# Latent queries summed in half a bank without a join, rotary halves shuffled, and three early tiles of the first gate

## The chip, the cores and the metric

One core of one Trainium2 chip runs the whole program. The metric is the device time of one execution, in microseconds. Before the change it is 2838.24 us, the median of 3 runs (2837.36 to 2838.51).

## The reference

A bidirectional encoder of two layers over 256 tokens of width 2048, in f32. Each layer projects the normed input into queries, keys and values of a differential attention, into two low-rank latents and a shared rotary key of a latent attention, and into two gates. Cut to what the change touches:

```python
h = rmsnorm(x, g_mix[i])
z = h @ w_in[i]
dq, dk, dv, cq, ckv, kr, ga, gb = jnp.split(z, split_at, axis=-1)
# differential attention: 8 heads -> od -> y_diff
qf = (rmsnorm(cq, g_q_latent[i]) @ w_q_up[i]).reshape(b, s, MLA_HEADS, 128 + 64)
q_nope = qf[..., :128]
q_rope = apply_rope(qf[..., 128:], cos_m, sin_m)
...
k_rope = apply_rope(kr[:, :, None, :], cos_m, sin_m)[:, :, 0, :]
om = latent_attention(q_nope, q_rope, k_nope, k_rope, v_mla)
merged = jax.nn.sigmoid(ga) * y_diff + jax.nn.sigmoid(gb) * y_mla
x = x + merged @ w_out[i]
# then a SwiGLU block and a gated embedding block
```

`apply_rope` rotates the first half of the 64 rotary features against the second half.

## The kernel before, in words

**Products.** Activations lie with features on the 128 partitions and the 256 tokens (`T`) along them, and every matmul operand is kept as a high and a low part: `u[:, :T]` and `u[:, T:]`. A weight tile comes by DMA in pieces of 8 blocks of 128 x 128 (`piece`); the scalar engine (ACT) rounds it into `whi`, the vector engine (DVE) writes the rest into `wlo`. `emit` then issues two matmuls for a block: `whi` against all 512 columns of the operand (high and low part side by side, into both halves of a PSUM bank), and `wlo` against the 256 high columns, into the second half. So the result lies in two halves, and `joined` adds them: ACT copies the second half into a scratch `join`, DVE adds the first half and writes a scratch `a` (four buffers). From then on the bank is free.

**Banks.** Products take one of four banks named `mm` (values `mmv` take the same four); transposes, small products and head outputs take two banks named `at`; scores take two banks named `S`.

**Latent queries.** `queries_up(n)` makes two tiles of `w_q_up` from one piece (`pair`), each from 4 blocks. Tiles 0 to 7 are the heads' unrotated parts; each is split into the operand `qn[n]`, which lies in the slot `fa(n)`. That slot holds the output `od[n]` of differential head n until `settle` has scaled and transposed it (a product with `ident` into an `at` bank, then a split into `ub`). Tiles 8 to 11 hold the rotary parts of two heads each; `rotated` multiplies them with a 128 x 128 matrix `swap` on the tensor engine (PE) to exchange the halves. The shared key goes through `swaps` and `halves` in the same way.

**Settling.** `settle(4)` scales `od[4]` to `od[7]`. Its factor is computed for the four heads at once by `rsqrt`, a chain of eleven small DVE operations (`rv`, `ry`, `ra`) on the sums of squares `ssd`, so it starts when head 7 is done.

**Gates.** 16 tiles of each gate (`wga`, `wgb`), 16 blocks each, fill PE's time beside the heads of the latent attention: two before each next head, `wga` there, `wgb` after it. Tile n of the first gate is stored in the slot `fa(n // 2)`, when the head's query that lies there has been used.

**Order.** All this is written as a program in order; a scheduler then puts each engine's instructions into a fixed order. Each engine works its own list strictly in that order, so an instruction that waits holds up all that stand behind it on its engine.

Of the kernel before, what the change touches and what calls it, by code (L numbers as in the profile page):

```python
# [12 lines left out]
F32 = mybir.dt.float32  # L13
# [26 lines left out]
BOTH = 6  # L40
PAD = 96 - 64 - 8
STEP = 48
NO_SYNC = mybir.DependencyInfo(mybir.DependencyClass.NoSync, mybir.DependencyReason.DATA)

TWO_PI = 2.0 * math.pi
# [8 lines left out]
def encoder(ctx, tc, x, p, positions, cols, lams, wq, wk, wv, wcq, wckv, wkr, wga, wgb,  # L54
            w_q_up, w_kn, w_v, w_bd, w_bm, w_out, w_gate, w_up, w_down, w_pin, w_pg, rope_c, out):
    nc = tc.nc
    V, A, PE = nc.vector, nc.scalar, nc.tensor
# [13 lines left out]
    def bank(ps=ps_at, tag="at", name="at", shape=(P, 2 * T)):  # L71
        return ps.tile(list(shape), F32, tag=tag, name=name)

    def tt(o, a, b, op):
        return V.tensor_tensor(out=o, in0=a, in1=b, op=op)  # L75
# [26 lines left out]
    at = 0  # L102
# [16 lines left out]
    swap, swaps, halves = (rc[:, 4 + j * P : 4 + (j + 1) * P] for j in range(3))  # L119
    aside = [fa(j) for j in range(5)]  # L120
    posi = aside[0][:, 0, :].bitcast(I32)
    posf = aside[0][:, 1, :]
# [86 lines left out]
    def emit(acc, hi, lo, at, us, first, last, inside=None):  # L209
        for j, u in enumerate(us):  # L210
            s, start, stop = slice((at + j) * P, (at + j + 1) * P), first and j == 0, last and j == len(us) - 1
            lead = PE.matmul(acc, hi[:, s], u, start=start, stop=False)  # L212
# [3 lines left out]
            rest = PE.matmul(acc[:, T:], lo[:, s], u[:, :T], start=False, stop=stop)  # L216
            if inside and inside[0] == j:
                tc.keep_in_program_order(rest)
# [9 lines left out]
            emit(acc, hi, lo, 0, us[a : a + m], a == 0, a + m == n, inside and (inside[0] - a, inside[1]))  # L228
        return acc

    def pair(src, us):

        n = len(us)
        hi, lo = piece(src.rearrange("n p m -> p n m"), 2 * n)
        for j in range(2):
            acc = bank(ps_mm, "mm", "mm")
            emit(acc, hi, lo, j * n, us, True, True)
            yield acc

    def joined(acc, o=None):  # L240
        t = scratch("join", 3)
        A.activation(t, acc[:, T:], AF.Copy)  # L242
        o = scratch("a", 4) if o is None else o
        tt(o, acc[:, :T], t, ALU.add)
        return o

    def split(u, src, gain=None):
        hi, lo = u[:, :T], u[:, T:]
        if gain is None:
            return A.activation(hi, src, AF.Copy), tt(lo, src, hi.bitcast(F32), ALU.subtract)  # L250
        return A.activation(hi, src, AF.Copy, scale=gain), stt(lo, src, gain, hi.bitcast(F32), ALU.mult, ALU.subtract)
# [109 lines left out]
        nc.gpsimd.memset(t.bitcast(F32), 0.0)  # L361

    def rotated(a, c_, s_, o=None):
        r = bank()
        if o is None:
            PE.matmul(r[:, T:], halves, a, start=True, stop=True)
        PE.matmul(r[:, :T], swap if o is not None else swaps, a, start=True, stop=True)  # L367
        t = scratch("sh", 2)
        tt(t, r[:, :T], s_, ALU.mult)
        tt(a, a if o is not None else r[:, T:], c_, ALU.mult)  # L370
        tt(a, a, t, ALU.add)
        if o is None:
            for j, t in enumerate(krs):
                split(t[64 * j : 64 * j + 64], a[64 * j : 64 * j + 64])
        else:
            split(o, a)
# [59 lines left out]
        return tmp.tile([P, 2, T], dt, tag=tag, name=tag, bufs=2)  # L436

    last_exp = [None]
    ROPE16 = [(j + 8) if j < 8 else (j - 8) if j < 16 else j for j in range(32)]

    def values(src, us, load=None):
# [43 lines left out]
    for L in range(DEPTH):  # L485
# [64 lines left out]
                split(kn[-1], joined(acc))  # L550

        def queries_up(n):
            for acc in pair(w_q_up[L, n : n + 2], cq):
                if n < MH:
                    qn.append(operand(fa(len(qn), F32R)))
                    split(qn[-1], joined(acc))
                else:
                    if n > MH:
                        qr.append(operand(fc(len(qr) - 2, F32R)))
                    at = qr[len(qr) - 1] if n > MH else qr[ropes[0]]  # L560
                    rotated(joined(acc), cos_m, sin_m, at)
                    ropes[0] += 1

        ropes = [0]
# [8 lines left out]
        def beside():  # L573

            for h in range(2, DH):
                if h < 6:
                    keys_up(2 * h - 4)
                elif h == 7:
                    rotated(joined(narrow(wkr[L], ua)), crm, srm)
                yield  # L580
                queries_keys(h)
                yield
            settle(0)
            for n in (8, 0, 2, 10):
                queries_up(n)
                yield
            settle(4)
            for n in (4, 6):
                queries_up(n)

        def gate(w, store, n):
            tt(store(n), joined(product(w[L, n], ua)), R, ALU.mult)

        def gate_a(n):
            if n % 2 == 0:
                gas.append(fa(n // 2))
            return gas[n // 2][:, n % 2, :]

        def gate_b(n):
            if n % 2 == 0:  # L600
                gbs.append(fb(n // 2))
            return gbs[n // 2][:, n % 2, :]

        gas, gbs = [], []

        def sigmoid(sg):
            si = A.activation(sg, sg, AF.Sigmoid)
# [57 lines left out]


        oms = ub[8:]
        todo = iter(range(NC))

        def mla_weights(h):  # L670
            E = weights()
            S, = scores(three(qn[h], kn[h]) + three(qr[h // 2], krs[h % 2]))
# [16 lines left out]
                    PE.matmul(o[:, :T], a[:, kb, :], b[:, kb, :], start=kb + j == 0, stop=kb + j == 3)  # L689
            split(oms[h], o[:, :T])  # L690

        pipelined(mla_weights, mla_out, MH, lambda: gate(wga, gate_a, next(todo)))


        for n in range(NC):
            gate(wgb, gate_b, n)
        ms = ua
        for n in range(NC):
            ga, gb = (t[n // 2][:, n % 2, :] for t in (gas, gbs))
# [186 lines left out]
        ("g_q_latent0", 4), ("g_q_latent1", 4), ("g_kv_latent0", 2), ("g_kv_latent1", 2), ("g_subln", 2)]  # L886


def rope_constants():


    c = np.zeros((P, 4 + 3 * P), np.float32)
    f32 = np.float32
    for base, dim in ((0, 16), (2, 64)):
        inv = f32(THETA) ** (-np.arange(0, dim, 2, dtype=f32) / f32(dim))
        for q in range(P):
            d = q % 64
            if d < dim:
                c[q, base] = inv[d % (dim // 2)]
                c[q, base + 1] = -1.0 if d < dim // 2 else 1.0  # L900
    for q in range(P):
        c[q, 4 + (q ^ 32)] = 1.0
        for m in (q, q ^ 64):
            c[q, 4 + P + (m ^ 32)] = 1.0
            c[q, 4 + 2 * P + m] = 1.0
    return c


# [18 lines left out]
def laid_out(a):  # L927
    a = {k: np.asarray(v) for k, v in a.items()}
    w_in = a["w_in"]
    cut = np.cumsum([0, 1024, 1024, 1024, QR, KVR, 64, DM, DM])  # L930
    z = [w_in[:, :, cut[j] : cut[j + 1]] for j in range(8)]
    up = a["w_q_up"].reshape(DEPTH, QR, MH, 192)
    kv = a["w_kv_up"].reshape(DEPTH, KVR, MH, 256)
    flat = lambda w: w.reshape(w.shape[0], w.shape[1], -1)
    named = {f"{n}{i}": a[n][i] for n in ("g_mix", "g_ffn", "g_ple", "g_q_latent", "g_kv_latent") for i in range(DEPTH)}
    named["g_final"] = a["g_final"]
    named["g_subln"] = a["g_subln"]
    return {
        "x": np.ascontiguousarray(a["x"][0].T.reshape(NC, P, T).transpose(1, 0, 2)),
        "p": np.ascontiguousarray(a["p"][:, 0].transpose(0, 2, 1).reshape(DEPTH, 2, P, T).transpose(0, 2, 1, 3)),  # L940
        "positions": np.ascontiguousarray(a["positions"]),
        "cols": np.ascontiguousarray(np.concatenate([columns(named[n]) for n, _ in COLS], axis=1)),
        "lams": np.ascontiguousarray(np.stack([a["lambda_q1"], a["lambda_q2"], a["lambda_k1"], a["lambda_k2"]], axis=1).reshape(1, -1)),
        "wq": tiles(z[0]), "wk": tiles(z[1]), "wv": wide(z[2]), "wcq": tiles(z[3]), "wckv": tiles(z[4]),
        "wkr": np.ascontiguousarray(z[5].reshape(DEPTH, NC, P, 64).transpose(0, 2, 1, 3)).reshape(DEPTH, P, NC * 64), "wga": tiles(z[6]), "wgb": tiles(z[7]),
        "w_q_up": tiles(np.concatenate([flat(up[..., :128]), flat(up[..., 128:])], axis=2)),
        "w_kn": tiles(flat(kv[..., :128])), "w_v": wide(flat(kv[..., 128:])),
        "w_bd": tiles(a["w_branch_diff"]), "w_bm": tiles(a["w_branch_mla"]), "w_out": tiles(a["w_out"]),
        "w_gate": tiles(a["w_gate_up"][:, :, :DFF]), "w_up": tiles(a["w_gate_up"][:, :, DFF:]),
        "w_down": tiles(a["w_down"]), "w_pin": tiles(a["w_ple_in"]), "w_pg": tiles(a["w_ple_gate"]),  # L950
        "rope_c": rope_constants(),
    }
# [17 lines left out]
```

## Time and profile before

| | |
|---|---|
| median of 3 runs | 2838.24 us (2837.36 to 2838.51) |
| profiled execution | 2838.84 us, its span 2837.0 us |
| TensorE (PE) busy | 2826.8 us, 100% of the span |
| VectorE (DVE) busy | 2073.0 us, 73% |
| ScalarE (ACT) busy | 1527.5 us, 54% |
| DMA | 531.49 MB, mean 187 GB/s |
| granted TensorE clock | 0.999 |

A row of the timeline has the start in us, then the duration, the engine, the line, the operation, what it writes and reads, the count of equal instructions merged into the row, and, in brackets, idle time ahead of it and what ended that. A matmul's duration has its passage through the array in it, and the next one starts long before it is over; so what a matmul costs PE is the distance from its start to the start of the next. The same holds, less strongly, for DVE and ACT. The two layers run the same program; the places named here are those of the first layer, whose latent queries stand at 200 to 222 us.

### The profile page before, as it was taken

The page shows a single profiled execution, that of the slowest core. Times are in us where ns is not written, and L with a number is a line of the kernel's source. Part 1 is how long each engine was busy: PE and PEld are TensorE (multiplying, and loading weights), DVE is VectorE, ACT ScalarE, POOL GpSimd, SP SyncE. Part 2 cuts the span into 40 slices and gives each one's busy share as a digit, 9 for nine tenths or more (in the row PEclk, how much of TensorE's full clock was granted, in tenths as well). Part 3 has the DMA queues.
Part 4 walks back from the last instruction along what each step waited for, and adds up shares of the span by engine and source line. Part 5 has one row for each costly group of instructions (what it writes and reads, how often), then busy time and mean ns, then how long its engine had stood idle before and what let it go on. Part 6 is the DMA issues. An engine that isn't in the chain of part 4 may idle for free.

```text
span 2837.0 us, 44038 instructions
## 1 busy us (share of the span) xinstructions
PE 2826.8 (100%) x16743; PEld 2498.5 (88%) x16743; DVE 2073.0 (73%) x3537; ACT 1527.5 (54%) x2548; POOL 1.9 (0%) x15
## 2 busy tenths in 40 slices
PE   9999999999999999999999999999999999999998
PEld 7888888888888888888888888888888888888888
DVE  7997658776666766677869976687766666666777
ACT  6676545554444444455646755555544444444556
POOL 0000000000000000000000000000000000000000
PEclk9999999999999999999999999999999999999999
DMA  7544466666665566566665445666666656666664
GB/s 244 169 161 149 162 194 197 192 194 193 187 199 193 182 198 201 194 193 194 193 192 169 155 150 168 195 197 194 193 193 187 199 193 187 202 194 194 193 193 155
DMA packets 156596, 531.49 MB, mean 187 GB/s; under 512 B 16992, under 2 KB 24160, under 8 KB 156384
## 3 DMA queue, kind: packets, MB, share of 16 engines
q1 hardware_dynamic: 155952, 528.09, 58.9%
q8 instruction: 131, 2.15, 0.3%
q14 instruction: 81, 0.66, 0.1%
q10 hardware_dynamic: 432, 0.59, 0.1%
HBM read 526.52 MB, written 2.10 MB: 186 GB/s over the span
## 4 chain that ended last, share of the span: by engine, by line
PE 99%; DMA 1%; DVE 0%; ACT 0%; issue 0%; SPq 0%; DVEq 0%; ACTq 0%
PE mm L212 61%; PE mm L216 31%; PE S L406 1%; PE mmv L462 1%; PE mmv L460 1%; PE mmv L461 1%; DMA w<-in_wv 1%; PE at L424 1%; PE at L632 1%; PE at L689 0%; PE mm L776 0%; PE mm L392 0%; DVE wlo L75 0%; PE at L647 0%; DVE a L75 0%; PE at L367 0%
## 5 line engine op out<-in xcount | busy, mean ns | idle before, releaser
L187 ACT ACTIVATE whi<-w 128x1024 fp32r<-128x1024 f32 (+2 forms) x1030 | 1063.1, 1033 | 1241.4 <-issue 704.3
L75 DVE TENSOR_TENSOR wlo<-w,whi 128x1024 fp32r<-128x1024 f32 (+2 forms) x1030 | 1224.4, 1189 | 676.5 <-ACT whi L187 667.8
L212 PE MATMUL mm<-ub,whi 128*128 128x512 f32 x3936 | 1342.3, 390 | 0.3
L212 PE MATMUL mm<-ua,whi 128*128 128x512 f32 x3712 | 1271.4, 390 | 0.0
L216 PE MATMUL mm<-ub,wlo 128*128 128x256 f32 x3936 | 1085.1, 276 | 0.0
L216 PE MATMUL mm<-ua,wlo 128*128 128x256 f32 x3712 | 1027.3, 277 | 0.0
L212 PEld LDWEIGHTS mm<-ub,whi 128*128 128x128 f32 x3936 | 738.2, 188 | 153.1 <-DVE a L75 0.7
L212 PEld LDWEIGHTS mm<-ua,whi 128*128 128x128 f32 x3712 | 696.0, 188 | 142.0
L216 PEld LDWEIGHTS mm<-ub,wlo 128*128 128x128 f32 x3936 | 738.8, 188 | 1.1
L216 PEld LDWEIGHTS mm<-ua,wlo 128*128 128x128 f32 x3712 | 696.9, 188 | 2.4 <-DVE wlo L75 0.6
L75 DVE TENSOR_TENSOR a<-mm,join 128x256 f32<-128x256 f32 (+1 forms) x423 | 175.1, 416 | 1.6 <-ACT join L805 1.4
L242 ACT ACTIVATE join<-mm 128x256 f32<-128x256 f32 x452 | 166.5, 370 | 5.2 <-PE mm L216 4.8
L75 DVE TENSOR_TENSOR xT<-xT,mm 128x256 f32<-128x256 f32 x256 | 106.8, 420 | 41.5 <-PE mm L216 37.7
L75 DVE TENSOR_TENSOR a<-a,row 128x256 f32<-128x256 f32 (+1 forms) x209 | 87.5, 422 | 5.9
L75 DVE TENSOR_TENSOR a<-a 128x256 f32<-128x256 f32 x120 | 50.8, 425 | 4.0
L460 PE MATMUL mmv<-whi,ua 128*128 128x512 f32 x128 | 50.1, 395 | 1.7 <-ACT whi L187 1.7
L75 DVE TENSOR_TENSOR ua<-a,ua 128x256 fp32r<-128x256 f32 x120 | 49.9, 417 | 1.0 <-ACT ua L250 1.0
L461 PE MATMUL mmv<-whi,ua 128*128 128x512 f32 x128 | 49.6, 391 | 0.0
L250 ACT ACTIVATE ua<-a 128x256 fp32r<-128x256 f32 x120 | 48.2, 403 | 2.6 <-DVE a L75 2.6
L415 ACT ACTIVATE E<-S,nm 128x256 f32<-128x256 f32 x96 | 44.2, 472 | 2.1 <-DVE nm L81 2.0
L462 PE MATMUL mmv<-wlo,ua 128*128 128x512 f32 x128 | 43.8, 393 | 0.1
L75 DVE TENSOR_TENSOR ssq<-ssq,sq 128x256 f32<-128x256 f32 x96 | 40.1, 417 | 0.3 <-ACT sq L280 0.3
(195 smaller groups left out, 1209.8 us busy)
## 6 DMA issues: line engine op xcount, KB each, us to landing
w<-in_w_gate SPq DMA_DIRECT2D x176, 512.0 KB, 4.7
w<-in_w_up SPq DMA_DIRECT2D x176, 512.0 KB, 4.7
w<-in_w_down SPq DMA_DIRECT2D x128, 512.0 KB, 4.1
w<-in_wga SPq DMA_DIRECT2D x64, 512.0 KB, 3.8
w<-in_wgb SPq DMA_DIRECT2D x64, 512.0 KB, 4.1
w<-in_w_out SPq DMA_DIRECT2D x64, 512.0 KB, 4.6
w<-in_w_pg SPq DMA_DIRECT2D x64, 512.0 KB, 4.7
w<-in_w_down SPq DMA_DIRECT2D x64, 384.0 KB, 3.7
```

Of the source, the lines that this page charges most:

```text
L75: return V.tensor_tensor(out=o, in0=a, in1=b, op=op)
L187: last_split[:] = A.activation(hi[:, :m], w[:, :m], AF.Copy), tt(lo[:, :m], w[:, :m], hi[:, :m].bitcast(F32), ALU.subtract)
L212: lead = PE.matmul(acc, hi[:, s], u, start=start, stop=False)
L216: rest = PE.matmul(acc[:, T:], lo[:, s], u[:, :T], start=False, stop=stop)
L242: A.activation(t, acc[:, T:], AF.Copy)
L250: return A.activation(hi, src, AF.Copy), tt(lo, src, hi.bitcast(F32), ALU.subtract)
L406: PE.matmul(S[:, b, :], q[:, b * P : (b + 1) * P], k, start=j == 0, stop=j == len(pairs) - 1)
L415: last_exp[0] = A.activation(E[:, b, :], S[:, b, :], AF.Exp, bias=nm[:, b : b + 1], scale=scale, accum_out=sm[:, b : b + 1])
L424: PE.transpose(tp[:, kb, b * P : (b + 1) * P], W[:, b, kb * P : (kb + 1) * P], ident)
L460: PE.matmul(banks[half][b], xh, hi[:, s], start=a + j == 0, stop=False)
L461: PE.matmul(banks[half][b], xl, hi[:, s], start=False, stop=False)
L462: last_mm[:] = [PE.matmul(banks[half][b], xh, lo[:, s], start=False, stop=a + j == n - 1)]
```

## The change

Four things:

1. The latent queries' products (`pair(..., True)`) run as three matmuls of 256 columns for a block: `whi` against the low part, `whi` against the high part, `wlo` against the high part, all summed in the first half of the bank. There is no join: `split` and `rotated` read the bank itself.
2. The rotary features are stored in another order (`LATENT_ORDER`), in which the two halves lie 16 partitions apart within each 32. `rotated` exchanges them with a DVE stream shuffle, so the products with `swap` and `swaps` are gone; `halves`, which copies the shared key to both halves of the partitions, stays.
3. A tile of the first gate is written ahead of the query tiles 4 and 5, one ahead of 6 and 7, and one behind them, all after `settle(4)`. They have buffers of their own (`early0` to `early2`).
4. The fill of the latent attention goes on from tile 3, and after the 16 tiles of the first gate takes tiles of the second.

```diff
-    def pair(src, us):
+    def pair(src, us, one=False):
...
-            emit(acc, hi, lo, j * n, us, True, True)
+            if one:
+                acc = acc[:, :T]
+                for k, u in enumerate(us):
+                    s = slice((j * n + k) * P, (j * n + k + 1) * P)
+                    for i, (w, x_) in enumerate(((hi, u[:, T:]), (hi, u[:, :T]), (lo, u[:, :T]))):
+                        PE.matmul(acc, w[:, s], x_, start=k + i == 0, stop=k + i == n + 1)
+            else:
+                emit(acc, hi, lo, j * n, us, True, True)
             yield acc
...
     def rotated(a, c_, s_, o=None):
-        r = bank()
         if o is None:
-            PE.matmul(r[:, T:], halves, a, start=True, stop=True)
-        PE.matmul(r[:, :T], swap if o is not None else swaps, a, start=True, stop=True)
+            r = bank()[:, :T]
+            PE.matmul(r, halves, a, start=True, stop=True)
+        else:
+            r, a = a, scratch("a", 4)
         t = scratch("sh", 2)
-        tt(t, r[:, :T], s_, ALU.mult)
-        tt(a, a if o is not None else r[:, T:], c_, ALU.mult)
+        V.stream_shuffle(t, r, SWAP16)
+        tt(t, t, s_, ALU.mult)
+        tt(a, r, c_, ALU.mult)
         tt(a, a, t, ALU.add)
...
+    SWAP16 = [(j + 16) % 32 for j in range(32)]
...
-            for acc in pair(w_q_up[L, n : n + 2], cq):
+            for acc in pair(w_q_up[L, n : n + 2], cq, True):
                 if n < MH:
                     qn.append(operand(fa(len(qn), F32R)))
-                    split(qn[-1], joined(acc))
+                    split(qn[-1], acc)
...
-                    rotated(joined(acc), cos_m, sin_m, at)
+                    rotated(acc, cos_m, sin_m, at)
...
             for n in (4, 6):
+                gate(wga, gate_a, next(todo))
                 queries_up(n)
+            gate(wga, gate_a, next(todo))
...
         def gate_a(n):
-            if n % 2 == 0:
+            if n < FIRST:
+                return gate_tile(n)
+            if n % 2 == 0 or n == FIRST:
                 gas.append(fa(n // 2))
-            return gas[n // 2][:, n % 2, :]
+            return gas[-1][:, n % 2, :]
...
-        pipelined(mla_weights, mla_out, MH, lambda: gate(wga, gate_a, next(todo)))
+        pipelined(mla_weights, mla_out, MH, fill_gate)
...
-        for n in range(NC):
-            gate(wgb, gate_b, n)
+        for n in todo:
+            gate(wgb, gate_b, n - NC)
```

The change moves instructions on every engine between the seventh differential head and the start of the latent heads. Outside of that stage, and after the gates, PE's list is the same. Two places follow; the numbers in the names tell instances apart.

**First place: the end of the queries.** On DVE before, the tiles 4 and 5 of the queries, in the banks `mm_2763` and `mm_2779`, stand in this order:

```order
L78 SCALAR_TENSOR_TENSOR E_2520<-E1_2521,rsum_2546,E_2520 128x256 x2
L75 TENSOR_TENSOR ub15_107<-a_2510,ub15_107 128x256
L75 TENSOR_TENSOR a_2775<-mm_2763,join_2773 128x256
L75 TENSOR_TENSOR a_2791<-mm_2779,join_2789 128x256
L412 TENSOR_REDUCE nm_2892<-S_2879 128x2
```

They are read into scratch `a` as soon as they are there, and their splits into `fa4` and `fa5` stand 46 rows further down. On DVE in the changed program the reader of tile 4's bank, now `mm_2814`, stands here; `fa4_2221` is head 4's output in the slot that the query takes over, `ub4` its transposed operand, `ry` the factor of `settle(4)`:

```order
L422 TENSOR_REDUCE nm_3266<-S_3253 128x2
L79 SCALAR_TENSOR_TENSOR ry_2716<-ra_2717,ry_2716 128x8
L76 TENSOR_TENSOR wlo_2990<-w32_2989,whi_2991 128x1024
L82 TENSOR_SCALAR nm_3266<-nm_3266 128x2
L82 TENSOR_SCALAR fa4_2221<-fa4_2221,ry_2716 128x128 x2
L82 TENSOR_SCALAR fa5_2426<-fa5_2426,ry_2716 128x128 x2
L82 TENSOR_SCALAR fa6_2607<-fa6_2607,ry_2716 128x128 x2
L82 TENSOR_SCALAR fa7_2711<-fa7_2711,ry_2716 128x128 x2
L422 TENSOR_REDUCE nm_3412<-S_3399 128x2
L79 SCALAR_TENSOR_TENSOR ub4_96<-at_2729,gsub_132,ub4_96 128x256
L76 TENSOR_TENSOR fa4_2827<-mm_2814,fa4_2827 128x256
```

The last row is the first that lets a query's bank go; it moved from ahead of the settling to behind all of it. On PE in the changed program, the third early gate tile `mm_2936` comes here, after the scores of the latent heads 0 to 3 (`S_3399` are those of head 3) and three of the transposes of `settle(4)`:

```order
L416 MATMUL S_3399<-kr1_136,ub15_107 128x256 x3
L672 MATMUL at_2729<-ident_112,fa4_2221 128x128 x2
L672 MATMUL at_2736<-ident_112,fa5_2426 128x128 x2
L672 MATMUL at_2743<-ident_112,fa6_2607 128x128 x2
L213 MATMUL mm_2936<-ua0_76,whi_2939 128x512
L217 MATMUL mm_2936<-ua0_76,wlo_2938 128x256
```

In the program before, the values' products and two gate tiles stand between the last output of a differential head and these transposes. The bank that `mm_2936` gets is the one that `mm_2814` had. The four banks at that point belong to `mm_2814`, `mm_2830`, `mm_2903` and `mm_2919`, the queries 4 to 7.

**Second place: the start of the queries.** On DVE before, the second rotary tile's bank `mm_2499` is read by the row with `a_2510`:

```order
L78 SCALAR_TENSOR_TENSOR E_2265<-E1_2266,rsum_2291,E_2265 128x256 x2
L75 TENSOR_TENSOR wlo_2657<-w32_2656,whi_2658 128x1024
L75 TENSOR_TENSOR a_2510<-mm_2499,join_2508 128x256
L75 TENSOR_TENSOR fa7_636<-a_2412,fa7_636 128x256
L75 TENSOR_TENSOR a_2582<-mm_2570,join_2580 128x256
```

On DVE in the changed program the same bank is read twice, by a shuffle and by the product with the cosine in `a_2512`:

```order
L76 TENSOR_TENSOR a_2491<-mm_2478,cos_m_601 128x256
L426 RECIPROCAL rsum_2291<-sm_2290 128x2
L76 TENSOR_TENSOR sh_2414<-sh_2414,fc0_623 128x256
L76 TENSOR_TENSOR a_2412<-a_2412,fc0_623 128x256
L76 TENSOR_TENSOR sh_2492<-sh_2492,sin_m_602 128x256
L82 TENSOR_SCALAR rsum_2291<-rsum_2291,neg_lam_131 128x2
L76 TENSOR_TENSOR a_2412<-a_2412,sh_2414 128x256
L76 TENSOR_TENSOR a_2491<-a_2491,sh_2492 128x256
L79 SCALAR_TENSOR_TENSOR E_2265<-E1_2266,rsum_2291,E_2265 128x256 x2
L76 TENSOR_TENSOR wlo_2657<-w32_2656,whi_2658 128x1024
L378 STREAM_SHUFFLE sh_2513<-mm_2499 128x256
L76 TENSOR_TENSOR a_2512<-mm_2499,cos_m_601 128x256
```

The rotary work of the first tile moved ahead of the piece `wlo_2657`. The next product to take this bank is query tile 3, `mm_2633`.

More of the change, by code (lines that the diff above doesn't have):

```diff
@@ L42 @@
 STEP = 48
+FIRST = 3
 NO_SYNC = mybir.DependencyInfo(mybir.DependencyClass.NoSync, mybir.DependencyReason.DATA)
@@ L118, in encoder @@
         nc.gpsimd.memset(times[:, k : k + 1], 64.0 * 0.25 ** (k % 3) * (EPS if k > 2 else 1.0 / DM))
-    swap, swaps, halves = (rc[:, 4 + j * P : 4 + (j + 1) * P] for j in range(3))
+    halves = rc[:, 4 : 4 + P]
     aside = [fa(j) for j in range(5)]
@@ L594, in gate_a, with gate_tile @@
         def gate_a(n):
-            if n % 2 == 0:
+            if n < FIRST:
+                return gate_tile(n)
+            if n % 2 == 0 or n == FIRST:
                 gas.append(fa(n // 2))
-            return gas[n // 2][:, n % 2, :]
+            return gas[-1][:, n % 2, :]
+        def gate_tile(n):
+            if n == len(early):
+                early.append(stat.tile([P, T], F32, tag=f"early{n}", name=f"early{n}", bufs=1))
+            return early[n]
         def gate_b(n):
@@ L602, in gate_b, with fill_gate @@
             return gbs[n // 2][:, n % 2, :]
-        gas, gbs = [], []
+        gas, gbs, early = [], [], []
+        todo = iter(range(2 * NC))
+        def fill_gate():
+            n = next(todo)
+            gate(*((wga, gate_a, n) if n < NC else (wgb, gate_b, n - NC)))
         def sigmoid(sg):
@@ L667, in encoder @@
         oms = ub[8:]
-        todo = iter(range(NC))
         def mla_weights(h):
@@ L690, in mla_out @@
             split(oms[h], o[:, :T])
-        pipelined(mla_weights, mla_out, MH, lambda: gate(wga, gate_a, next(todo)))
-        for n in range(NC):
-            gate(wgb, gate_b, n)
+        pipelined(mla_weights, mla_out, MH, fill_gate)
+        for n in todo:
+            gate(wgb, gate_b, n - NC)
         ms = ua
         for n in range(NC):
-            ga, gb = (t[n // 2][:, n % 2, :] for t in (gas, gbs))
+            ga = early[n] if n < FIRST else gas[n // 2 - FIRST // 2][:, n % 2, :]
+            gb = gbs[n // 2][:, n % 2, :]
             sigmoid(ga)
@@ L886 @@
         ("g_q_latent0", 4), ("g_q_latent1", 4), ("g_kv_latent0", 2), ("g_kv_latent1", 2), ("g_subln", 2)]
+LATENT_ORDER = [q // 32 * 16 + q % 16 + q % 32 // 16 * 32 for q in range(64)]
 def rope_constants():
-    c = np.zeros((P, 4 + 3 * P), np.float32)
+    c = np.zeros((P, 4 + P), np.float32)
     f32 = np.float32
@@ L896, in rope_constants @@
         for q in range(P):
-            d = q % 64
+            d = q % 64 if dim < 64 else LATENT_ORDER[q % 64]
             if d < dim:
@@ L901, in rope_constants @@
     for q in range(P):
-        c[q, 4 + (q ^ 32)] = 1.0
         for m in (q, q ^ 64):
-            c[q, 4 + P + (m ^ 32)] = 1.0
-            c[q, 4 + 2 * P + m] = 1.0
+            c[q, 4 + m] = 1.0
     return c
@@ L944, in laid_out @@
         "wq": tiles(z[0]), "wk": tiles(z[1]), "wv": wide(z[2]), "wcq": tiles(z[3]), "wckv": tiles(z[4]),
-        "wkr": np.ascontiguousarray(z[5].reshape(DEPTH, NC, P, 64).transpose(0, 2, 1, 3)).reshape(DEPTH, P, NC * 64), "wga": tiles(z[6]), "wgb": tiles(z[7]),
-        "w_q_up": tiles(np.concatenate([flat(up[..., :128]), flat(up[..., 128:])], axis=2)),
+        "wkr": np.ascontiguousarray(z[5][:, :, LATENT_ORDER].reshape(DEPTH, NC, P, 64).transpose(0, 2, 1, 3)).reshape(DEPTH, P, NC * 64), "wga": tiles(z[6]), "wgb": tiles(z[7]),
+        "w_q_up": tiles(np.concatenate([flat(up[..., :128]), flat(up[..., 128:][..., LATENT_ORDER])], axis=2)),
         "w_kn": tiles(flat(kv[..., :128])), "w_v": wide(flat(kv[..., 128:])),
```

## The prediction

> **What bounds the kernel now.** The page comes first: busy time by engine, and the chain that ended last.
>
> ```profile
> PE 2826.8 (100%) x16743; PEld 2498.5 (88%) x16743; DVE 2073.0 (73%) x3537; ACT 1527.5 (54%) x2548; POOL 1.9 (0%) x15
> PE 99%; DMA 1%; DVE 0%; ACT 0%; issue 0%; SPq 0%; DVEq 0%; ACTq 0%
> ```
>
> PE is busy all the time and carries 99% of the chain, so a microsecond counts only where it is taken from PE's list or where PE is made to wait. DVE at 73% is no bound on the average, but the stage of the queries is not the average: there DVE works without a pause. So I read the timeline of that stage, PE first.
>
> ```profile
> 213.16 0.60 PE L367 MATMUL at<-a,rc 128*128 128x256 f32 x2
> 213.41 0.58 PE L212 MATMUL mm<-ub,whi 128*128 128x512 f32 x1
> 213.83 0.28 PE L216 MATMUL mm<-ub,wlo 128*128 128x256 f32 x1
> 213.95 0.40 PE L212 MATMUL mm<-ub,whi 128*128 128x512 f32 x1
> 214.18 0.28 PE L216 MATMUL mm<-ub,wlo 128*128 128x256 f32 x1
> 214.29 0.39 PE L212 MATMUL mm<-ub,whi 128*128 128x512 f32 x1
> ...
> 217.52 0.59 PE L406 MATMUL S<-fb,fa 128*128 128x256 f32 x3
> 218.26 0.50 PE L212 MATMUL mm<-ub,whi 128*128 128x512 f32 x1
> ```
>
> Starts are what counts. A block of a query costs a pair of matmuls, from 213.95 to 214.29: 0.34 us. A product with `swap` (L367, two passes in f32) with the 512-column matmul behind it takes from 213.16 to 213.83, 0.67 us, of which the matmul alone needs 0.23 (213.95 to 214.18): the swap costs 0.44 us. And three score matmuls take from 217.52 to 218.26, 0.74 us, where about 0.36 is their own (0.12 each, below): PE waits some 0.3 us. That is the only wait of note in the stage, and the second layer is taken to have the same.
>
> **The change, part by part.** All terms are for both layers and are added to the profiled execution, 2838.84 us (span 2837.0 and 1.84 around it); it lies 0.6 us over the median of the runs, 2838.24, so the sum is then put on the median.
>
> *Swaps gone.* Four for the queries and one for the key in each layer, 10 in all, 0.43 to 0.44 us each: −4.3 us. `halves` stays.
>
> *Three matmuls of 256 in place of 512 and 256.* The head outputs (L689) are of exactly this kind: three products for a block, two of them with the same weights.
>
> ```profile
> 260.06 0.76 PE L689 MATMUL at<-wt,E 128*128 128x256 f32 x5
> 260.66 0.60 PE L424 MATMUL at<-ident,E 128*128 128x128 f32 x4
> ```
>
> Five in 0.60 us, 0.12 each, so a block costs 0.36 instead of 0.34 to 0.35. There are 12 tiles of 4 blocks in each layer, 96 blocks: 96 × 0.015 = +1.5 us. By the Trainium skill, TensorE: Matmul & The Clock Gate, section Back-to-back issue gap, a matmul costs its columns at 2.4 GHz and 2.5 ns more. By that an estimate of the term would be only 96 × 2.5 ns = +0.2 us. The rows of this case show 0.12 us for 256 columns behind 256, and they are used.
>
> *Joins gone.* 24 ACT copies and 24 DVE additions; both engines lie beside PE. That is worth nothing by itself, but with them goes a place to put a result: before, a product left its bank for a scratch `a` at once. Now the bank is held until the query's own slot `fa(n)` is free, which is after `settle` has used the head output that lies there. This gives two waits.
>
> *The wait at the end of the queries.* By the order in front of this, `mm_2936`, the third early gate tile, takes the bank of `mm_2814` and must wait for the row `fa4_2827`, and all four product banks are held by the queries 4 to 7. What PE has between head 7's last output product and this tile are 3 + 12 score matmuls, the last query tile with 12, and 24 more score matmuls: 51 × 0.12 = 6.1 us, and six transposes. How long the chain takes from the same moment comes from these rows:
>
> ```profile
> 220.00 1.05 PE L632 MATMUL at<-vals,wt 128*128 128x128 f32 x8
> 220.81 0.48 PE L212 MATMUL mm<-ub,whi 128*128 128x512 f32 x1
> ...
> 221.09 0.39 ACT L635 ACTIVATE fa<-at 128x256 f32<-128x256 f32 x1
> ...
> 222.16 0.18 ACT L637 ACTIVATION_READ_ACCUMULATOR fa<-fa 128x1 f32 x1
> ...
> 223.43 0.69 DVE L412 TENSOR_REDUCE nm<-S 128x2 f32<-128x512 f32 x1 [0.83 <-PE S L406]
> 224.04 1.22 DVE L75 TENSOR_TENSOR wlo<-w,whi 128x1024 fp32r<-128x1024 f32 x1
> 225.17 0.16 DVE L81 TENSOR_SCALAR nm<-nm 128x2 f32<-128x2 f32 x1
> ...
> 226.63 0.62 DVE L81 TENSOR_SCALAR E<-E,rsum 128x256 f32<-128x256 f32 x2
> 227.16 0.42 DVE L75 TENSOR_TENSOR fc<-a,fc 128x256 fp32r<-128x256 f32 x1
> ...
> 235.90 0.17 DVE L78 SCALAR_TENSOR_TENSOR ry<-ra,ry 128x8 f32<-128x8 f32 x1
> 236.10 0.17 DVE L78 SCALAR_TENSOR_TENSOR ra<-ry 128x8 f32<-128x8 f32 x1
> ...
> 238.39 1.65 DVE L81 TENSOR_SCALAR fa<-fa,ry 128x128 f32<-128x128 f32 x8
> 239.97 1.23 DVE L75 TENSOR_TENSOR wlo<-w,whi 128x1024 fp32r<-128x1024 f32 x1
> ...
> 244.15 0.48 DVE L78 SCALAR_TENSOR_TENSOR ub<-at,gsub,ub 128x256 fp32r<-128x256 f32 x1
> 244.54 0.41 DVE L75 TENSOR_TENSOR fa<-a,fa 128x256 fp32r<-128x256 f32 x1
> ```
>
> Head 6 shows that ACT has the sums of squares 1.5 us after PE is through with the output product (220.81 to 222.34). Then the chain on DVE: eleven small operations at 0.20 us (235.90 to 236.10), and between them, in the fixed order, one reduction at 0.61 us (223.43 to 224.04) and four scalings of `E` at 0.27 (two from 226.63 to 227.16): 1.5 + 2.2 + 0.6 + 1.1 = 5.4 us, less some 0.4 us where a small operation's latency is used by a scaling: 5.0 us. From there the eleven rows of the order run without a gap: the scores' reduction 0.6 (its matmuls are done 4.7 us after the start, 39 × 0.12, so it does not wait), the small one 0.2, the piece `wlo_2990` 1.13 (224.04 to 225.17), eight scalings of `fa` 1.6 (238.39 to 239.97), the second reduction 0.6, `ub4` 0.4 (244.15 to 244.54) and `fa4` 0.4, with 0.1 for the small `nm`: 5.0 us. So the bank is free 10.0 us after the start. PE has 6.1 us of work and the six transposes, which lie inside the wait, 0.65 us (six at 0.11; the eight of the L632 rows take 0.81). Left over is a wait of 10.0 − 6.1 − 0.65 = 3.3 us in each layer, +6.6 us. What is queued behind the waiting matmul on PE is all the rest. Nothing is ready: every product needs a bank.
>
> *The wait at the start of the queries.* Query tile 3 (`mm_2633`) takes the bank that the second rotary tile leaves by `a_2512`.
>
> ```profile
> 200.37 0.48 PE L212 MATMUL mm<-ub,whi 128*128 128x512 f32 x1
> ...
> 202.17 0.44 DVE L524 STREAM_SHUFFLE sh<-a 128x256 f32<-128x256 f32 x1
> 202.66 0.17 DVE L416 RECIPROCAL rsum<-sm 128x2 f32<-128x2 f32 x1
> ...
> 206.75 0.42 DVE L75 TENSOR_TENSOR a<-mm,join 128x256 f32<-128x256 f32 x1
> 207.09 0.42 DVE L75 TENSOR_TENSOR fa<-a,fa 128x256 fp32r<-128x256 f32 x1
> ```
>
> Before, the bank was read at 206.75 and free at 207.2. Now DVE has ahead of that point a shuffle of 0.49 (202.17 to 202.66) and two multiplications and an addition of 0.34 (206.75 to 207.09) for a join of 0.34, and 0.15 more for the key's shuffle: +1.3 us; the reading itself is a shuffle and a multiplication, +0.5; and DVE gains 0.6 where it waited before, for the key's swap and for ACT. So the bank is free at about 208.4. PE began the queries at 200.37; one swap earlier, now, and five tiles of 12 × 0.12 and four transposes later, it is at 207.4 and waits 1.0 us: +2.0 us for both layers. Its lower end is nothing, its upper end 1.7 us a layer, if DVE gains nothing.
>
> *Waits that go.* The 0.3 us at 217.8, where DVE was late with joins: −0.6 us. After a wait PE's first matmul is 0.1 us longer (0.33 from 218.26 to the next start, for 0.23), four times: +0.4 us.
>
> *Early tiles, the later fill, shorter constants.* The same gate products at other times. They fill what would be a longer wait, but the third comes too late for it, since it needs a bank itself. No cost, no gain: behind them PE's list is that of before.
>
> Sum: −4.3 + 1.5 + 6.6 + 2.0 − 0.6 + 0.4 = +5.6 us. On the median that is 2843.8; I say 2844.0 us, for the gaps of some hundredths that no row shows singly. Of a change under 0.2%, 5.7 us, the measurement could hardly tell that there is one.
>
> **The rivals.** *No bank is waited for* (the other side). If DVE runs the settling chain in 6.7 us, the bank is free when PE comes, and only the swaps and the triples are left: −4.3 + 1.5 − 0.6 = −3.4, 2834.8 us. It decides at DVE's list: without the reductions and scalings of the scores and the piece, the chain would be 1.5 + 2.2, the first scaling, a transpose, `ub4` and `fa4`, below 6.1. Against it stands that DVE takes them in the order shown. For it: the order was made by a scheduler that may see the chain shorter. 0.11.
>
> *One wait only, or half of both.* DVE is freed of 24 joins and may come to the place early; then the sum is +1 to +3, about 2841.0 us. 0.10.
>
> *The clock falls in the long wait.* PE is nearly idle for 4 us. Rows that bear on it:
>
> ```profile
> 1.05 3.78 PE L476 MATMUL at<-ones 128*128 128x128 f32 x16 [1.05 <-DVE ones L115]
> ...
> 22.00:24.00 2.00, 0.32 (x2) 0.29 (x2) 0.30 (x1) 1.39 (x3) 0.00 (x0) 1.00 0.85 254
> 2830.00:2831.40 1.40, 0.00 (x0) 0.00 (x0) 1.26 (x5) 1.36 (x3) 0.00 (x0) 1.00 0.78 291
> 2831.40:2836.00 4.60, 0.00 (x0) 0.00 (x0) 0.82 (x2) 0.74 (x2) 0.00 (x0) 0.50 0.86 342
> ```
>
> The windows give PE's busy time second and the granted clock third from the end. A wait of 1.7 us at 22 us left the clock at 1.00; behind the last matmul it fell to 0.50 within 1.5 us. The first sixteen matmuls, of the transposes' shape, took 3.78 us, 0.24 each instead of 0.11. If the clock falls, about as long a stretch runs at half speed and loses some 1.8 us, 3.6 us for both layers: 2847.6 us. Against it: six transposes lie in the gap and cut it into pieces of about 1.5 us. The Trainium skill, TensorE: Matmul & The Clock Gate, Part 1, says that the clock is halved after an idle window of about 3.4 us and comes back after as long a busy one. By that rule this rival has its chance from where the window falls; both ends of this trace agree with a halving, neither shows its window. 0.17.
>
> *Faster by over 5.7 us.* All that can be taken from PE here is 4.9 us, so it needs something that no row shows. 0.05.
>
> **How the numbers follow.** The forecast, both waits about as sized, has 0.57. Its own range, with 2.5 to 4 us and 0.5 to 1.5 us a layer for the two waits, is 2841.5 to 2847; about three fifths of it lie above 2843.9, where slower by over 0.2% begins. Slower: 0.57 × 0.61 + 0.17 = 0.52. Within 0.2%: 0.57 × 0.39 + 0.11 + 0.10 = 0.43. Faster: 0.05. The range takes in all named cases but the last: 2834.5 to 2849.5 us.
>
> **What would show it.** Right: no L367 rows; query matmuls of 256 columns at 0.12 us; in each layer a wait of about 3 us on PE at the third early gate tile, released by DVE's `fa` of L75 and cut by transposes, and one of about 1 us at query tile 3; the clock at 1.00 throughout. Wrong: PE's chain unbroken there, with the time under 2838; or the wait released by something else than the bank's reader; or matmuls of double length behind the wait, which is the clock.

## The result, and the profile after

| | before | after |
|---|---|---|
| median, 12 runs each | 2838.24 us (2837.16 to 2838.77) | 2844.61 us (2842.68 to 2846.73) |
| ratio | | 1.0024, 95% interval 1.0016 to 1.0031 |
| profiled execution | 2838.84 us | 2844.07 us, span 2842.2 |

The change costs 6.4 us, 0.24%. Busy time and the chain by engine after, from the page:

```profile
PE 2827.2 (99%) x16819; PEld 2501.0 (88%) x16819; DVE 2066.9 (73%) x3533; ACT 1520.1 (53%) x2524; POOL 1.9 (0%) x15
PE 97%; DVE 2%; DMA 1%; ACT 0%; issue 0%; DVEq 0%; SPq 0%; ACTq 0%
```

And PE's waits (what waits, for whom, us in total, times, longest):

```profile
PE at L672 <- DVE ub L79: 2.9, 2, 1.4
PE at L672 <- DVE fa L82: 1.7, 2, 0.9
PE mm L217 <- DVE wlo L76: 1.5, 2, 0.8
PE at L487 <- DVE ones L116: 1.1, 1, 1.1
PE mm L243 <- DVE a L76: 0.6, 2, 0.3
```

DVE's share of the chain went from 0 to 2%: PE waits for it where before it did not. The waits at L672 are those of the settling transposes; the table counts only idle time between modelled ends, so the starts of the timeline are needed for their size. PE first, then DVE, at the end of the queries in the first layer:

```profile
237.06 0.52 PE L416 MATMUL S<-fb,fa 128*128 128x256 f32 x3
237.41 0.52 PE L416 MATMUL S<-kr,ub 128*128 128x256 f32 x3
238.79 0.92 PE L672 MATMUL at<-ident,fa 128*128 128x128 f32 x4 [0.85 <-DVE fa L82]
241.15 0.44 PE L672 MATMUL at<-ident,fa 128*128 128x128 f32 x2 [1.44 <-DVE ub L79]
241.48 0.50 PE L213 MATMUL mm<-ua,whi 128*128 128x512 f32 x1
241.81 0.28 PE L217 MATMUL mm<-ua,wlo 128*128 128x256 f32 x1
```

```profile
237.18 0.15 DVE L79 SCALAR_TENSOR_TENSOR ry<-ra,ry 128x8 f32<-128x8 f32 x1
237.25 1.22 DVE L76 TENSOR_TENSOR wlo<-w,whi 128x1024 fp32r<-128x1024 f32 x1
238.38 0.16 DVE L82 TENSOR_SCALAR nm<-nm 128x2 f32<-128x2 f32 x1
238.46 1.65 DVE L82 TENSOR_SCALAR fa<-fa,ry 128x128 f32<-128x128 f32 x8
240.02 0.68 DVE L422 TENSOR_REDUCE nm<-S 128x2 f32<-128x512 f32 x1
240.62 0.47 DVE L79 SCALAR_TENSOR_TENSOR ub<-at,gsub,ub 128x256 fp32r<-128x256 f32 x1
241.02 0.41 DVE L76 TENSOR_TENSOR fa<-mm,fa 128x256 fp32r<-128x256 f32 x1
```

PE's scores are done at 237.77 (237.41 and 3 x 0.12), the third early gate tile starts at 241.48. Less 0.65 for the six transposes, PE waits 3.1 us. DVE works through the eleven rows of the order without a gap (the first, a reduction, starts at 236.57), and the very last, the split of query tile 4 out of its bank, ends at about 241.4, right ahead of the gate tile. PE's idle time itself lies at the transposes: until 238.79 they wait for the scaled head output (`fa` of L82), and until 241.15 the third of them waits for one of the two `at` banks (`ub` of L79). At the gate tile no idle time is left.

The clock (PE's busy time is the second number, the granted clock the third from the end) during the wait and behind it, in both layers:

```profile
237.70:241.50 3.80, 1.50 (x9) 0.80 (x8) 3.80 (x14) 1.39 (x4) 0.00 (x0) 1.00 0.39 134
241.50:245.00 3.50, 3.50 (x21) 3.06 (x21) 1.45 (x5) 1.33 (x3) 0.00 (x0) 1.00 0.02 7
1648.05:1651.85 3.80, 1.51 (x9) 0.80 (x8) 3.80 (x14) 1.39 (x4) 0.00 (x0) 1.00 0.41 138
1652.40:1655.90 3.50, 3.50 (x13) 2.95 (x12) 0.88 (x4) 0.31 (x2) 0.00 (x0) 0.51 0.00 0
```

The two waits are alike to 0.01 us of busy time, yet only behind the second did the clock fall, for about 3.4 us from 1652.4 on.

A measure that leaves the start and the clock out is the period of a layer: from the first scores of head 0 in the first layer to those in the second. Before, and after:

```profile
109.30 0.97 PE L406 MATMUL S<-fa,ub 64*128 64x256 f32 x12
1517.45 0.97 PE L406 MATMUL S<-fa,ub 64*128 64x256 f32 x12
```

```profile
108.25 0.97 PE L416 MATMUL S<-fa,ub 64*128 64x256 f32 x12
1518.91 0.98 PE L416 MATMUL S<-fa,ub 64*128 64x256 f32 x12
```

1408.15 us before, 1410.66 after: +2.51 us a layer, +5.0 for two. The first scores come 1.05 us earlier after, but they lie anywhere from 108.2 to 109.4 us over the kernels below, so that is not put down to the change. From the second layer's row to the end of the span after needs 1323.3 us, the kernel with copied banks below 1318.9 (2835.4 - 1516.46): 4.4 us more, where in the first layer the difference is 3.07. The 1.3 us between the two is put down to the clock: in the two windows of 3.5 us behind the waits PE got through 13 matmuls in place of 21.

### The profile page after: what moved, and what is told of

Its sections match the earlier page's. It is cut to its first block, busy times and chain, and to the rows that moved or that the text cites. A ratio compares the mean times of both kernels' runs of the same rounds, so it can differ in the third digit from the quotient of the medians.

```text
span 2842.2 us, 44152 instructions
## 1 busy us (share of the span) xinstructions
PE 2827.2 (99%) x16819; PEld 2501.0 (88%) x16819; DVE 2066.9 (73%) x3533; ACT 1520.1 (53%) x2524; POOL 1.9 (0%) x15
## 4 chain that ended last, share of the span: by engine, by line
PE 97%; DVE 2%; DMA 1%; ACT 0%; issue 0%; DVEq 0%; SPq 0%; ACTq 0%
PE mm L213 60%; PE mm L217 30%; PE mmv L471 1%; PE mmv L473 1%; PE mmv L472 1%; PE S L416 1%; PE mm L243 1%; DVE wlo L76 1%; PE at L434 0%; PE at L657 0%; PE at L712 0%; PE mm L800 0%; DMA w<-in_wv 0%; PE mm L402 0%; DVE a L76 0%; DMA xT<-in_x 0%
## 5 line engine op out<-in xcount | busy, mean ns | idle before, releaser
L213 PE MATMUL mm<-ub,whi 128*128 128x512 f32 x3840 | 1307.0, 389 | 0.0
L217 PE MATMUL mm<-ub,wlo 128*128 128x256 f32 x3840 | 1058.4, 276 | 0.0
L217 PE MATMUL mm<-ua,wlo 128*128 128x256 f32 x3712 | 1027.8, 277 | 1.5 <-DVE wlo L76 1.5
L213 PEld LDWEIGHTS mm<-ub,whi 128*128 128x128 f32 x3840 | 720.3, 188 | 148.9
L217 PEld LDWEIGHTS mm<-ub,wlo 128*128 128x128 f32 x3840 | 720.8, 188 | 1.0
L217 PEld LDWEIGHTS mm<-ua,wlo 128*128 128x128 f32 x3712 | 697.8, 188 | 3.9 <-DVE wlo L76 2.1
L76 DVE TENSOR_TENSOR a<-mm,join 128x256 f32<-128x256 f32 x399 | 165.4, 416 | 12.0 <-ACT join L250 10.5
L250 ACT ACTIVATE join<-mm 128x256 f32<-128x256 f32 x428 | 156.0, 366 | 3.1 <-PE mm L217 2.8
```

## The experiments

The kernels below "after" were timed in five rounds beside the kernel before, whose medians there were 2838.41 and 2838.30 us. Periods are read as above.

| kernel | median us | ratio to before | period us | against before |
|---|---|---|---|---|
| before | 2838.3 to 2838.4 | | 1408.15 | |
| after | 2844.61 | 1.0024 (1.0016 to 1.0031) | 1410.66 | +2.51 |
| shuffles alone | 2837.28 | 0.9995 (0.9986 to 1.0004) | 1407.57 | -0.58 |
| copied banks | 2837.45 | 0.9997 (0.9988 to 1.0005) | 1407.59 | -0.56 |
| gates first | 2841.32 | 1.0010 (1.0001 to 1.0018) | 1409.37 | +1.22 |
| no early tiles | 2856.01 | 1.0061 (1.0047 to 1.0075) | 1415.51, a fall of the clock in it | +7.36 |
| shuffles, early tiles | 2835.62 | 0.9992 (0.9983 to 1.0001) | 1406.97 | -1.18 |
| copied banks, spaced sigmoids | 2834.86 | 0.9988 (0.9979 to 0.9996) | 1406.52 | -1.63 |
| shuffles, early tiles, spaced sigmoids | 2833.68 | 0.9985 (0.9976 to 0.9994) | 1405.91 | -2.24 |
| triples copied, no early tiles | 2834.26 | 0.9986 (0.9978 to 0.9995) | 1406.03 | -2.12 |

The intervals of shuffles alone, of copied banks and of shuffles with early tiles take in 1: by their times alone they can't be told from the kernel before. There the argument rests on the periods, each read from one profiled execution, and on the waits.

**Is the long wait the held bank?** Copied banks: the kernel after, with

```diff
+    def copied(acc):
+        o = scratch("a", 4)
+        A.activation(o, acc, AF.Copy)
+        return o
...
-                    split(qn[-1], acc)
+                    split(qn[-1], copied(acc) if n > 2 else acc)
```

and the early tiles joined in their own buffers, so that the four `a` are free for the queries.

> The kernel after, but ScalarE copies the banks of query tiles 4 to 7 to scratch tiles, so that no bank is held until a head output is settled. If the held banks are the cause: the wait at the third early tile goes, with it 3.3 us a layer and the stretch at half clock; 2844.6 - 6.6 - about 1 = 2837 us (2836 to 2839). Rival, that the three matmuls of 256 or the early tiles themselves cost the time: 2843 or more.

Measured 2837.45 us. PE's waits:

```profile
PE mm L217 <- DVE wlo L76: 1.5, 2, 0.8
PE at L492 <- DVE ones L116: 1.1, 1, 1.1
PE mmv L476 <- ACT whi L188: 1.1, 2, 0.7
PE mm L243 <- DVE a L76: 0.7, 2, 0.3
```

The waits at the transposes are gone. The row with `mmv` is new, but its two waits lie in the loading at the start (6.6 and 28.8 us) and outside of the period. The period falls by 3.07 us, which is the 3.1 us read from the starts, and the median by 7.2 us: two waits, and about 1 us of clock. The matmuls and the early tiles stay in this kernel, so they are not what makes the long wait. Since the scheduler knows that the bank is free, it also orders PE's work otherwise. The third early tile now starts straight behind the last query tile, and the transposes of the settling come 10 us later:

```profile
233.03 0.39 PE L213 MATMUL mm<-ua,whi 128*128 128x512 f32 x1
243.49 0.60 PE L678 MATMUL at<-ident,fa 128*128 128x128 f32 x4
```

So what is shown is the held bank together with the order that follows from it: with no bank free, PE has nothing that could stand ahead of the transposes. In the order of the kernel after, the third transpose would have held PE until 241.15 even if the bank had been free. There a free bank alone could have saved 0.1 us at most: from 241.15 to the gate tile it is 0.33, and the two transposes take 0.22 of that.

**Does the wait follow PE's cover?** Gates first: all three early tiles ahead of query tiles 4 to 7.

```diff
-            for n in (4, 6):
-                gate(wga, gate_a, next(todo))
-                queries_up(n)
-            gate(wga, gate_a, next(todo))
+            for _ in range(FIRST):
+                gate(wga, gate_a, next(todo))
+            for n in (4, 6):
+                queries_up(n)
```

> The kernel after, but with all three early gate tiles ahead of query tiles 4 to 7. Held banks as the cause: behind head 7's output PE now has 67 matmuls of 0.12 us, 8.0 us in place of 6.1, and VectorE's chain takes about 9.8 us, so the wait shrinks from 3.3 to 1.1 to 1.5 us a layer, now ahead of the values' products; too short for the clock to fall: 2844.6 - 4 - 1 = 2839.5 us (2838 to 2841.5). Rival, that the wait is set by VectorE's own list whatever PE does: 2844 as before.

2841.32 us, inside the range, 1.8 us above the 2839.5 named. The wait is still there, shorter, and now ahead of the values (`mmv`):

```profile
242.48 0.44 PE L672 MATMUL at<-ident,fa 128*128 128x128 f32 x2 [1.61 <-DVE ub L79]
242.81 0.50 PE L471 MATMUL mmv<-whi,ub 128*128 128x512 f32 x1
```

By the period it is 1.8 us a layer (1409.37 against 1407.59 with copied banks), 0.3 to 0.7 more than expected. DVE's chain, from the end of head 7's outputs at 232.3 to the end of the query's split at 242.7, took 10.4 us for the 9.8 expected; behind the start of the settling two weight pieces of 1.13 us stand in it, at 236.23 and 240.15, where the kernel after has one. The idle time again ends with `ub`, the row ahead of that split.

No early tiles: `FIRST = 0`, and the gate calls between the queries left out.

> The kernel after without the early gate tiles (the fill as in the kernel before), the three matmuls and held banks kept. Held banks as the cause: only 12 score matmuls lie behind head 7's output, the wait is 5 to 6 us a layer, and the clock falls behind it in both layers; the 0.8 us wait at the end of the gates goes; 2850 us (2847 to 2854). Rival, that the early tiles bring the cost: about 2838.

2856.01 us: the direction is right, the size 6 us short. Two things were missed. Head 7's transposes and outputs and the scores behind them now also wait for the exponentials and what follows these, since nothing fills PE between them (4.8 us of idle time in both layers by PE's waits); and the clock, expected to fall once in a layer, fell twice in the second, each time for 6.8 us. Rows of PE there:

```profile
224.19 0.33 PE L434 MATMUL at<-ident,E 128*128 128x128 f32 x1 [1.30 <-DVE E L79]
224.92 0.62 PE L416 MATMUL S<-fb,fa 128*128 128x256 f32 x3 [0.40 <-ACT E L425]
```

And the clock behind these waits, in both layers:

```profile
222.10:225.50 3.40, 1.71 (x13) 1.31 (x12) 3.40 (x10) 1.32 (x5) 0.00 (x0) 1.00 0.48 166
225.50:228.90 3.40, 2.71 (x24) 2.48 (x23) 1.51 (x6) 1.60 (x6) 0.00 (x0) 1.00 0.16 65
1637.60:1640.90 3.30, 1.61 (x12) 1.21 (x12) 3.30 (x10) 1.33 (x5) 0.00 (x0) 1.00 0.45 159
1640.90:1644.30 3.40, 2.71 (x15) 2.31 (x13) 1.34 (x4) 0.70 (x2) 0.00 (x0) 0.51 0.22 76
```

So the early tiles are no cost at this place: they are the cover that keeps the held banks from costing more.

**What are the shuffles worth?** Shuffles alone: from the kernel after, `pair` without the third argument, `split(qn[-1], joined(acc))`, `rotated(joined(acc), ...)`, which then works in place, no early tiles.

> The shuffled halves alone, on the kernel before: queries of 512 and 256 columns with their joins, the fill of the gates as before. If the swap products are worth what their starts showed (10 at 0.43 to 0.44 us) and the shuffles hide on VectorE: 2838.2 - 4.3 = 2833.9 us, within 2833 to 2835, and no wait of over 0.5 us on PE between the rotary tiles and the end of the queries. Rival, that the shuffles make VectorE the one that is late there: PE waits for VectorE near the queries, and the time is above 2836.

2837.28 us, where 2833.9 was expected and above 2836 was the rival: the rival holds. In PE's waits there is a new row of six, and the second of them shows in the timeline:

```profile
PE mm L213 <- DVE a L76: 2.2, 6, 0.5
```

```profile
214.93 0.28 PE L217 MATMUL mm<-ub,wlo 128*128 128x256 f32 x1
215.75 0.51 PE L213 MATMUL mm<-ub,whi 128*128 128x512 f32 x1 [0.54 <-DVE a L76]
```

From start to start it is 0.82 us for a matmul of 0.11: 0.7 us. The two others of a layer, read in the same way, are 0.5 and 0.4. Beside the shuffles DVE is late with the joins, and the bank, which a join frees, comes late. The swaps' 2.15 us a layer, less 1.6 for these waits and 0.3 for restarts, plus the 0.4 that went at 217.8, leave 0.65; the period shows 0.58.

Shuffles and early tiles: the kernel after without the three matmuls.

> The kernel after without the three matmuls of 256: shuffles and the three early tiles, but queries of 512 and 256 columns that are joined and leave their bank at once. Theory (swaps gone 4.3 us; query tile 3 waits about 0.5 us a layer for VectorE; the early tiles give VectorE time for its joins; 15 sigmoids in a row at the end of the gates cost 0.8 us a layer): 2838.4 - 4.3 + 1.0 + 1.6 - 0.6 = 2836.1 us (2835 to 2837). Rival, that the joins beside the shuffles keep VectorE late as with the shuffles alone: 1.1 us a layer more, 2838.3 us.

2835.62 us: with a gate tile between the queries, only the first of the three waits is left (0.6 us in all in PE's table, 0.3 each). So DVE was late with the joins for want of room, and the early tiles give it room.

Triples copied: shuffles, three matmuls of 256, every query bank copied by ACT, no early tiles.

> Shuffles and the three matmuls of 256, every query bank copied by ScalarE to a scratch tile, no early tiles: against the shuffles alone (2837.3 us) it puts the three matmuls (96 blocks, 0.36 for 0.34 us: +1.5 us) and takes VectorE's 24 joins. If the matmuls cost 1.5 us and VectorE's lateness with joins cost 0.7 and 0.4 us a layer: 2837.3 + 1.5 - 2.2 = 2836.6 us. If the matmuls cost 0.2 us: 2835.3. If VectorE was not late through the joins: 2838.8.

2834.26 us, 2.3 us below the expectation for 1.5 us. None of the three waits is left, not even the one at query tile 3, since ACT frees the rotary banks, and the expectation had counted only two. With the third (0.5) and the restarts behind all of them (0.3) the waits are 1.9 us a layer: 2837.3 + 1.2 - 3.8 = 2834.7 us, 1.2 being the price of the matmuls that follows now.

**The new wait at the end of the gates.** PE's `mm L217 <- DVE wlo`, 0.8 us a layer, was in no term of the prediction. ACT's list in the second layer after, and PE's wait:

```profile
1753.68 1.28 ACT L632 ACT_TABLE_LOAD   x1
1754.98 1.03 ACT L632 ACTIVATE early<-early 128x256 f32<-128x256 f32 x3
1755.92 3.78 ACT L632 ACTIVATE fa<-fa 128x256 f32<-128x256 f32 x12
1759.61 0.36 ACT L250 ACTIVATE join<-mm 128x256 f32<-128x256 f32 x1
1759.87 1.05 ACT L188 ACTIVATE whi<-w 128x1024 fp32r<-128x1024 f32 x1
```

```profile
1760.97 0.49 PE L213 MATMUL mm<-ua,whi 128*128 128x512 f32 x1
1762.23 0.39 PE L217 MATMUL mm<-ua,wlo 128*128 128x256 f32 x1 [0.77 <-DVE wlo L76]
```

Fifteen sigmoids, everything that is ready when the last exponentials are done, stand ahead of a join and a weight piece. Before, they were thirteen, and PE's wait behind them was 0.24 us by the starts (331.97 to 332.44 for a matmul of 0.23). After, it is 1.03 by the starts (1760.97 to 1762.23), of which 0.77 shows as idle time. Spacing them tests it; in `sigmoid`, `spaced` being ACT's splits of the merged tiles so far:

```diff
-            tc.add_manual_dep(si.ins, last_exp[0].ins.name, NO_SYNC, reason="one change of tables")
+            for i in [last_exp[0]] + spaced[-2:-1]:
+                tc.add_manual_dep(si.ins, i.ins.name, NO_SYNC, reason="one change of tables")
...
-            split(ms[n], yd)
+            spaced.append(split(ms[n], yd)[0])
```

> The kernel with copied banks, and the sigmoids of the gates spaced: from the third tile on, each waits for ScalarE's split two tiles before, so that they don't stand in a row ahead of the last joins and weight pieces. If the row of 15 sigmoids is what delays the last gate's second piece: the wait of 0.8 us a layer goes, 2837.45 - 1.6 = 2835.8 us (2835 to 2836.5). Rival, that the piece is late for another reason or the sigmoids now come too late for their tiles: 2837.4 or more.

> Shuffles, early tiles with joined queries, and spaced sigmoids: what is left of the change when the held banks, the three matmuls and the row of sigmoids are out. By the theory 2836.1 - 1.6 = 2834.5 us (2833.5 to 2836), faster than both kernels; by the rival on VectorE 2836.7 us.

2834.86 us, 0.1 below its range, and 2833.68 us. In both the period falls by 1.07 us (1407.59 to 1406.52, 1406.97 to 1405.91), more than the 0.8 expected, which was the idle time alone; by the starts the wait was 1.03 us. The two kernels differ in the three matmuls with copies against 512 and 256 with joins, and their periods by 0.61 us: for 48 blocks that is 0.013 us a block, the price of a triple. The starts agree: over some 30 blocks a query's block takes 0.354 us in the kernel after and 0.343 in the kernel before. The kernel with joins is the best of all, 4.6 us below the kernel before and 10.9 below the kernel after. All that PE still waits for in it:

```profile
PE at L487 <- DVE ones L116: 1.1, 1, 1.1
PE mm L213 <- DVE a L76: 0.6, 2, 0.3
PE mmv L471 <- ACT whi L188: 0.3, 1, 0.3
```

## Why the prediction was right, and where only by its sum

2844.0 us was forecast, 2844.61 measured. Its terms, for one layer:

| term | forecast | measured | from |
|---|---|---|---|
| swaps gone | -2.15 | -2.15 | five swaps at 0.43 by their starts before; none after |
| triples | +0.75 | +0.61 | periods of the two spaced kernels; starts +0.55 |
| wait at the end of the queries | +3.3 | +3.1 | starts; copied banks 3.07 |
| wait at the start | +1.0 | +0.5 | starts |
| wait at 217.8 gone | -0.3 | -0.4 | 217.52 to 218.26, less 3 x 0.12; none after |
| restarts | +0.2 | +0.1 | 0.1 each at 206.97 and 241.48; the one at 218.26 went |
| row of sigmoids | 0 | +0.8 | 1.03 by the starts (spaced kernels 1.07), less 0.24 before |
| sum | +2.8 | +2.6 | period +2.51 |

- **The end of the queries** holds in size and place, and in its mechanism with one exception. From the end of head 7's output products (eight from 230.84, so 231.65) to the end of the row from 241.02, about 241.4, DVE's chain took 9.7 us for the 10.0 forecast, and PE's work was 6.1 for 6.1. But one sign of being wrong came: PE's wait was released by something else than the reader of the query's bank. The gate tile was to wait for that reader; in the trace it shows no idle time, and the transposes ahead of it wait, for the scaling (`fa` of L82) and for an `at` bank (`ub` of L79). The forecast reader is the DVE row behind that `ub`, 0.4 us later, so both bounds fall together, and the size came out right either way. Copied banks shows that the held bank is what brings PE to stand there.
- **The triples** cost 0.013 us a block for the 0.015 forecast. The formula of the Trainium skill (TensorE: Matmul & The Clock Gate, section Back-to-back issue gap), 2.5 ns more for a matmul, would have been 0.1 us a layer. The measurement, 0.61, is near the rows and far from that; the section itself gives the formula for an isolated matmul.
- **The start of the queries** was mis-sized by half. DVE's rows, and then PE's:

```profile
206.16 0.45 DVE L378 STREAM_SHUFFLE sh<-mm 128x256 f32<-128x256 f32 x1
206.51 0.41 DVE L76 TENSOR_TENSOR a<-mm,cos_m 128x256 f32<-128x256 f32 x1
206.83 0.47 DVE L79 SCALAR_TENSOR_TENSOR ub<-at,gsub,ub 128x256 fp32r<-128x256 f32 x1
```

```profile
206.37 0.28 PE L243 MATMUL mm<-ub,wlo 128*128 128x256 f32 x1
206.97 0.51 PE L243 MATMUL mm<-ub,whi 128*128 128x256 f32 x2 [0.32 <-DVE a L76]
```

  The bank is free at 206.9; with the 1.05 us by which everything lies earlier in this execution that is 207.9 for the 208.4 forecast, while PE comes at 207.5 for 207.4. (The forecast's own terms for PE add up to 207.6: 200.37 less 0.44, 60 x 0.12, and four transposes at 0.11.) DVE's side was taken as too slow. Part of that is known: a shuffle holds up the next full row for 0.35 us, and the 0.49 that was used is the distance to a small reciprocal behind a shuffle.
- **Early tiles at no cost** failed. At the place where they stand they are cover, as said; but with them and the later fill, fifteen sigmoids in place of thirteen stand in front of a gate's weights, on ACT, 110 us later. The kernels without early tiles have no such row in PE's waits (0.23 us by the starts with the shuffles alone), those with them have 1.03, until the sigmoids are spaced. The sentence that PE's list behind them is that of before was true, and did not reach ACT's.
- **The clock at 1.00** failed in one layer of two in the profiled execution, 1.3 us. The median's 6.4 us, less 5.0 from the periods, leave 1.4 us, which fits one such fall in an execution; only one execution was profiled. It was the rival given 0.17, at 1.8 us a layer; it came not instead of the forecast but on top of it, in part of the layers.

The other signs came as said: no swap product is left, and the query matmuls start 0.12 us apart. So the forecast put five terms 0.1 to 0.5 us a layer too high (the wait at the start, that at the end, the triples, the restarts, and the wait that goes) and left two out, the row of sigmoids (0.8 a layer) and the fall of the clock (1.4 in an execution). That these came out nearly even, and the time within 0.6 us, is luck; that the held banks bring the largest term is not. The rival on the other side, no bank waited for, is what copied banks show: 2837.45 us. It had been put at 2834.8, for want of the row of sigmoids and the wait at the start.

## What to carry to other kernels

A join or a copy that looks idle on its engine can be what frees a bank: before it is taken out, look what the new reader of the bank waits for, and count PE's work up to the next user of a bank against that chain. A product taken from PE and given to an engine that is late in the same stage is worth its time only when that engine gets room. And work that is done earlier is also ready earlier: see what the other engines then put in front of something urgent.

## What the runs showed of the hardware

Of waits that are alike, one halves TensorE's clock and another doesn't: 3.8 us with 1.5 us busy left it at 1.00 at 237.7 us, and at 1648 us brought it to 0.50 for 3.4 us, and in the kernel without early tiles 3.4 us with 1.7 us busy left it alone in the first layer and 3.3 us with 1.6 us busy halved it in the second, for 6.8 us (1641.0 to 1647.8). The Trainium skill, TensorE: Matmul & The Clock Gate, Part 1, has the clock set by a window of 3413 ns that runs freely. That agrees with the 3.4 us, and with 6.8 as twice that, and a free window would explain why the same wait falls differently; its rule of an idle window is met here by stretches in which PE was busy for two fifths to half of the time. How busy a window must be to keep the clock, no run here settles.
